# A two-layer encoder on one core: sums of the down projection moved from POOL to VectorE and to an accumulating DMA, residual added at the PSUM read, matmuls ordered bank by bank

## The chip, the cores and the metric

One core of a Trainium2 chip runs the whole program in one launch. The metric is the device time of the program in microseconds (us). The kernel before was timed in three runs: 2201.31, 2204.14 and 2206.15 us, median 2204.14 us.

## The reference, cut to what matters

Two encoder layers (a windowed attention in the first, a neighbourhood attention in the second, with memory heads beside them), each followed by a dense SwiGLU channel mixer. Everything is float32, with 1024 tokens, 1024 model columns and 2816 hidden columns. The change lies in the last product of the mixer:

```python
x = x + jnp.concatenate([y_tok, y_mem], axis=-1) @ w_out[i]
h = rmsnorm(x, norm_ffn[i])
gu = h @ w_gate_up[i]
x = x + (jax.nn.silu(gu[..., :D_FF]) * gu[..., D_FF:]) @ w_down[i]   # the down projection
```

After the second layer a final RMSNorm gives the output.

## The kernel before, in words

**Precision.** Each float32 operand is split into two reduced-precision parts: `hi` (a cast on ScalarE, ACT, L106) and `lo` (a subtraction on VectorE, DVE, L109). A product is then three matmuls: high by high, high by low, low by high (`three`).

**The down projection by seven products.** The product of a 1024x2816 weight and 2816x1024 activations is cut into halves in each direction and computed by a Strassen-like scheme of seven products instead of eight. Product `i` (0 to 6) takes a sum or difference of weight halves on the left (`left_side`) and a sum or difference of activation halves on the right. The right sides were already combined after the gate and up product, by `hand_over`, and stored to DRAM as `b_d[layer][i]` by `keep` (L963, L964). `right_side` (L1065) loads them again into `b_raw` and splits them into `hB`.

**Loops.** Each product runs over 11 row tiles `p` of the hidden dimension, taken in six groups `g` of two tiles (the last has one), and over four PSUM banks `m`. A tile and bank cost three matmuls of 128x128 by 512 columns, so a full group is 24 matmuls, one product is 132, and one layer's down projection is 924. The inner order is tile outside, bank inside, except in the last two groups, which go bank by bank (L1176 to L1187). The operands of a group are asked for two groups ahead (`dorder[at_ + 2]`).

**Weights.** `keep_rows` loads the first half-rows of the weight, both column halves, into six `wd_kept` tiles, 1 MB each (`a` and `b` are its two column halves). Product 1 needs `b` plus the second half-rows; these are loaded into a `wd_raw` tile and added on GpSimd (POOL, L1039), then DVE forms `a = b - a` (L1040). Product 3 loads two more halves and POOL subtracts them (L1061); product 5 loads one and POOL subtracts (L1050). The `wd_raw` and `xr` tiles share five slots; the split weights `wd` have three.

**Reading the banks.** At the end of products 0, 2, 3 and 4, `read` (L1094) copies each of the four banks to SBUF on ACT, loads the residual (`residual`, L1077, from `xr_d`), and adds it on POOL (L1096). In product 4 DVE also adds the copied bank to `x`. Products 1, 5 and 6 add straight from the bank on DVE. `done` squares finished tiles on ACT and sums the squares on DVE (L202) for the next RMSNorm; `scale` closes the sum with small matmuls (`st` L211, `bc` L226). In product 6 the norm of the first token half starts after group 0.

**Order.** The code is written in program order, and a scheduler lays out each engine's own instruction list from it ahead of the run: an instruction can stand earlier than its place in the text if its engine was thought to be free. On the chip each list runs strictly in order, and a list whose next instruction waits for data waits as a whole. SP issues nearly all the DMAs; ACT issues a few stores; POOL issues none.

Of the kernel before, what the change touches and what calls it, by code (L numbers as in the profile page):

```python
# [12 lines left out]
ALU = mybir.AluOpType  # L13
# [28 lines left out]
def trunk_kernel(ctx: ExitStack, tc: tile.TileContext, a: dict, out: bass.AP):  # L42
# [288 lines left out]
    for layer in range(2):  # L331
# [427 lines left out]
        with tc.tile_pool(name=f"fp{layer}", bufs=1, reuse_waits="tile") as fp:  # L759
# [203 lines left out]
            def keep(i, p, t):  # L963
                nc.sync.dma_start(b_d[layer][i][:, p * HS : (p + 1) * HS], t)  # L964
# [57 lines left out]
            def left_side(i, g):  # L1022
# [12 lines left out]
                elif i == 1:  # L1035
                    src, o = raw(), raw()
                    rows(src, g, 1, first_cols)
                    rows(o, g, 1, second_cols)
                    nc.gpsimd.tensor_tensor(b, b, o, op=ALU.add)  # L1039
# [7 lines left out]
                elif i == 5:  # L1047
                    src = raw()
                    rows(src, g, 1, first_cols)
                    nc.gpsimd.tensor_tensor(src, src, a, op=ALU.subtract)  # L1050
# [6 lines left out]
                if i == 3:  # L1057
                    r = raw()
                    rows(r, g, 0, first_cols)
                    rows(b, g, 0, second_cols)  # L1060
                    nc.gpsimd.tensor_tensor(b, r, b, op=ALU.subtract)  # L1061
# [15 lines left out]
            def residual(m, f):  # L1077
                t = raw_tile("xr")[:, :HS]
                nc.sync.dma_start(t, xr_d[layer][m][:, f * HS : (f + 1) * HS])
                return t  # L1080
# [13 lines left out]
            def read(i, m, bank):  # L1094

                add = lambda o, p_, q_, op=ALU.add, e=nc.vector: e.tensor_tensor(o, p_, q_, op=op)  # L1096
                if i == 0:
                    t = x_tile(m, 1)
                    nc.scalar.copy(t, bank)
                    add(t, t, residual(m, 1), e=nc.gpsimd)  # L1100
# [3 lines left out]
                elif i == 2:  # L1104
                    t = x_tile(m, 0)
                    nc.scalar.copy(t, bank)
                    add(t, t, residual(m, 0), e=nc.gpsimd)
                elif i == 3:
                    t = x_tile(m + 4, 0)
                    nc.scalar.copy(t, bank)  # L1110
                    add(t, t, residual(m + 4, 0), e=nc.gpsimd)
                elif i == 4:
                    t = x_tile(m + 4, 1)
                    nc.scalar.copy(t, bank)
                    add(x[m + 4][0], x[m + 4][0], t)
                    done(m + 4, 0)
                    add(t, t, residual(m + 4, 1), e=nc.gpsimd)
# [36 lines left out]
            for u, n in gate_up():  # L1154
                if u.j == NF - 1 and n in (2, 3, 4):
                    for g in (2 * n - 4, 2 * n - 3):
                        keep_rows(g)
                    if n > 2:
                        left_side(0, n - 3)
                        right_side(0, n - 3)  # L1160
# [4 lines left out]
            for at_, (i, g) in enumerate(dorder):  # L1165
                if at_ + 2 < len(dorder):
                    left_side(*dorder[at_ + 2])
                    right_side(*dorder[at_ + 2])
# [7 lines left out]
                if g == len(groups) - 1:  # L1176
                    for m in range(4):
                        product(i, m, p, bank[m])
                        read(i, m, bank[m])
                elif g == len(groups) - 2:  # L1180
                    for m in range(4):
# [105 lines left out]
```

## Time and profile before

| | us |
|---|---|
| median of three runs | 2204.14 |
| the profiled execution, its own time | 2205.49 |
| its span in the trace | 2202.5 |
| PE (TensorE matmuls) busy | 2129.8 (97%) |
| DVE busy | 1440.2 (65%) |
| ACT busy | 1056.5 (48%) |
| POOL busy | 673.9 (31%) |

The span is some 3 us less than the execution's own time. Line numbers (L1136) are those of the kernel before; a line can be a helper's. In a timeline row, "x39" means 39 merged instructions of one kind, and the bracket gives the engine's idle time ahead of them and what ended it. The down projection of the first layer runs from 850 to 1079 us of the span, that of the second from 1954 to 2181 us.

### The profile page before, as it was taken

The page shows a single profiled execution, that of the slowest core. Times are in us where ns is not written, and L with a number is a line of the kernel's source. Part 1 is how long each engine was busy: PE and PEld are TensorE (multiplying, and loading weights), DVE is VectorE, ACT ScalarE, POOL GpSimd, SP SyncE. Part 2 cuts the span into 40 slices and gives each one's busy share as a digit, 9 for nine tenths or more (in the row PEclk, how much of TensorE's full clock was granted, in tenths as well). Part 3 has the DMA queues.
Part 4 walks back from the last instruction along what each step waited for, and adds up shares of the span by engine and source line. Part 5 has one row for each costly group of instructions (what it writes and reads, how often), then busy time and mean ns, then how long its engine had stood idle before and what let it go on. Part 6 is the DMA issues. An engine that isn't in the chain of part 4 may idle for free.

```text
span 2202.5 us, 28160 instructions
## 1 busy us (share of the span) xinstructions
PE 2129.8 (97%) x9930; PEld 1749.9 (79%) x9930; DVE 1440.2 (65%) x2241; ACT 1056.5 (48%) x2016; POOL 673.9 (31%) x647
## 2 busy tenths in 40 slices
PE   6899999999999999999999999999999999999996
PEld 6688888788888887787788888887888888877875
DVE  5677787776555456767866666667865555567575
ACT  5477785443333333445466566653433333334442
POOL 4334330323332321363233233202233233213540
PEclk8999999999999999999999999999999999999998
DMA  6312117423223236766332222274232232366562
GB/s 221 119 39 82 49 58 268 133 82 122 97 93 110 100 115 225 248 208 215 111 91 72 76 65 86 64 263 139 82 101 110 96 115 96 120 225 229 178 234 81
DMA packets 117020, 287.21 MB, mean 130 GB/s; under 512 B 12304, under 2 KB 18704, under 8 KB 116880
## 3 DMA queue, kind: packets, MB, share of 16 engines
q1 hardware_dynamic: 110544, 273.89, 36.9%
q10 hardware_dynamic: 6336, 11.54, 1.4%
q8 instruction: 78, 1.28, 0.2%
q14 instruction: 62, 0.51, 0.1%
HBM read 210.40 MB, written 68.94 MB: 127 GB/s over the span
## 4 chain that ended last, share of the span: by engine, by line
PE 73%; issue 10%; DVE 6%; ACT 4%; DMA 4%; POOL 3%; SPq 0%; POOLq 0%; DVEq 0%; ACTq 0%
PE X L844 21%; PE Y L844 16%; PE mm L139 13%; PE X L1136 6%; PE po L139 4%; PE S L524 3%; PE Y L1136 3%; PE O L587 3%; PE pT L567 2%; DMA b_raw<-b_d 1%; DVE hB L109 1%; ACT p L539 1%; POOL x L1096 1%; DVE wd L109 1%; DMA wd_kept<-in_w_dn 1%
## 5 line engine op out<-in xcount | busy, mean ns | idle before, releaser
L844 PE MATMUL X<-hT,wgu 128*128 128x512 f32 x1056 | 259.0, 395 | 0.0
L844 PE MATMUL Y<-hB,wgu 128*128 128x512 f32 x1056 | 256.3, 392 | 0.0
L1136 PE MATMUL X<-hB,wd 128*128 128x512 f32 x1056 | 248.3, 395 | 7.0 <-DVE c L852 3.4
L844 PE MATMUL X<-hB,wgu 128*128 128x512 f32 x1056 | 247.8, 390 | 0.0
L1136 PEld LDWEIGHTS X<-hB,wd 128*128 128x128 f32 x1056 | 200.2, 190 | 52.9 <-DVE c L852 4.3
L844 PEld LDWEIGHTS X<-hT,wgu 128*128 128x128 f32 x1056 | 198.2, 188 | 47.2
L552 POOL TENSOR_SCALAR p<-p,stat 128x384 f32<-128x384 f32 (+1 forms) x256 | 140.9, 570 | 309.8 <-DVE stat L549 206.6
L844 PEld LDWEIGHTS Y<-hB,wgu 128*128 128x128 f32 x1056 | 198.5, 188 | 43.9 <-issue 1.5
L844 PEld LDWEIGHTS X<-hB,wgu 128*128 128x128 f32 x1056 | 198.3, 188 | 41.8
L106 ACT CAST wgu<-wS 128x1024 fp32r<-128x1024 f32 x88 | 92.5, 1051 | 259.7 <-POOL wS L803 157.1
L109 DVE TENSOR_TENSOR wgu<-wgu_raw,wgu 128x1024 fp32r<-128x1024 f32 (+1 forms) x88 | 85.7, 974 | 190.3 <-ACT wgu L106 190.3
L139 PE MATMUL mm<-hT,wqk 128*128 128x512 f32 x672 | 199.8, 405 | 0.1
L1136 PE MATMUL Y<-hB,wd 128*128 128x512 f32 x792 | 185.2, 395 | 8.9 <-DVE hB L109 4.5
L803 POOL TENSOR_TENSOR wS<-wgu_raw 128x512 f32<-128x512 f32 x44 | 73.6, 1672 | 379.0 <-DVE wgu L109 379.0
L139 PE MATMUL po<-yT,wo 128*128 128x512 f32 x768 | 184.7, 394 | 0.0
L1136 PEld LDWEIGHTS Y<-hB,wd 128*128 128x128 f32 x792 | 150.6, 191 | 42.6 <-DVE hB L109 5.3
L109 DVE TENSOR_TENSOR hB<-b_raw,hB 128x512 fp32r<-128x512 f32 x154 | 131.9, 892 | 53.1 <-ACT hB L106 52.9
L139 PEld LDWEIGHTS po<-yT,wo 128*128 128x128 f32 x768 | 142.4, 188 | 29.5 <-issue 1.0
L109 DVE TENSOR_TENSOR wgu<-wS,wgu 128x1024 fp32r<-128x1024 f32 x88 | 109.7, 1247 | 62.6 <-ACT wgu L106 62.6
L539 ACT ACTIVATE p<-p,stat 128x256 f32<-128x256 f32 (+1 forms) x192 | 112.4, 586 | 51.1 <-DVE stat L535 48.5
L810 POOL TENSOR_TENSOR wS<-wgu_raw 128x512 f32<-128x512 f32 x44 | 58.3, 1326 | 251.2 <-DMA wgu_raw<-in_w_gu 197.5
L106 ACT CAST hB<-b_raw 128x512 fp32r<-128x512 f32 x154 | 88.8, 619 | 95.4 <-DMA b_raw<-b_d 95.3
(158 smaller groups left out, 4026.8 us busy)
## 6 DMA issues: line engine op xcount, KB each, us to landing
wgu_raw<-in_w_gu SPq DMA_DIRECT2D x92, 512.0 KB
b_raw<-b_d SPq DMA_DIRECT2D x70, 512.0 KB
wd_raw<-in_w_dn SPq DMA_DIRECT2D x50, 512.0 KB
b_d<-c SPq DMA_DIRECT2D x88, 256.0 KB
b_d<-t SPq DMA_DIRECT2D x66, 256.0 KB
wo_raw<-in_w_out SPq DMA_DIRECT2D x32, 512.0 KB
wd_kept<-in_w_dn SPq DMA_DIRECT2D x10, 1024.0 KB
x<-in_x SPq DMA_DIRECT2D x32, 256.0 KB
```

Of the source, the lines that this page charges most:

```text
L106: nc.scalar.copy(dst, src)
L109: (eng or nc.vector).tensor_tensor(dst, src, h.bitcast(F32), op=ALU.subtract)
L139: nc.tensor.matmul(ps[:, :n], l, r, start=start and i == 0 and j == 0, stop=stop and i == len(order) - 1 and j == 2,)
L524: nc.tensor.matmul(s_[:, :n], Q[self.h][:, qb * P : (qb + 1) * P], k, start=j == 0, stop=j == 1)
L539: nc.scalar.activation(p[:, :n], p[:, :n], AF.Exp, bias=m1, scale=-1.0, accum_out=s1)
L552: nc.gpsimd.tensor_scalar(p[:, :n], p[:, :n], ri[:, i : i + 1], 1.0, op0=ALU.mult, op1=ALU.mult)
L567: nc.tensor.transpose(tr[:, j * P : (j + 1) * P], p[:, j * P : (j + 1) * P], ident)
L587: nc.tensor.matmul(o[:, c0 : c0 + w * P], self.value(j), t[:, s0 : s0 + w].rearrange("p j q -> p (j q)"), start=j == js[0] and t is self.p ...
L803: sub = lambda o, p_, q_: nc.gpsimd.tensor_tensor(o, p_, q_, op=ALU.subtract)
L810: nc.gpsimd.tensor_tensor(s[:, HS:], u1, u2, op=ALU.add)
L844: nc.tensor.matmul(ps, l, r, start=n in (0, 1, 3, 6) and k == 0 and i == 0, stop=k == 3 and i == 2, skip_group_check=True,)
L1136: nc.tensor.matmul(bank, l, r, start=i in (0, 1, 3, 6) and p == 0 and n == 0, stop=p == HF - 1 and n == 2, skip_group_check=True,)
```

## The change

1. `left_side`, product 1: the second half-rows are no longer loaded into a tile and added on POOL. A DMA issued from POOL's queue adds them into `b` while it writes (`accum_op=ALU.add`).
2. `left_side`, products 5 and 3: the two subtractions move from POOL to DVE.
3. `residual`: the residual tiles of four banks are loaded ahead, at group 3 of products 0, 2, 3 and 4, by two DMAs of two tiles each; the sixteen loads per layer become eight.
4. `read`: no copy on ACT and no addition on POOL. DVE adds bank and residual in one instruction. In product 4 DVE reads each bank twice.
5. `keep`: the seven stores of the last row tile (`p == HF - 1`) are issued from POOL's queue, not SP's.
6. The right side of product 0, group 2, is asked for inside the gate and up loop, with groups 0 and 1, and no longer after it.
7. Every group runs bank by bank (bank outside, tile inside).
8. In product 6 the norm of the first half starts after group 1, not 0, and the squares of the other half are added one group later.

```diff
             def keep(i, p, t):
-                nc.sync.dma_start(b_d[layer][i][:, p * HS : (p + 1) * HS], t)
+                queue = nc.gpsimd if p == HF - 1 else nc.sync
+                queue.dma_start(b_d[layer][i][:, p * HS : (p + 1) * HS], t)
...
                 elif i == 1:
-                    src, o = raw(), raw()
+                    src = raw()
                     rows(src, g, 1, first_cols)
-                    rows(o, g, 1, second_cols)
-                    nc.gpsimd.tensor_tensor(b, b, o, op=ALU.add)
+                    nc.gpsimd.dma_start(
+                        b, wd[p : p + n, 1].rearrange("n r c -> r n c")[:, :, second_cols], accum_op=ALU.add
+                    )
                     nc.vector.tensor_tensor(a, b, a, op=ALU.subtract)
...
                 elif i == 5:
                     src = raw()
                     rows(src, g, 1, first_cols)
-                    nc.gpsimd.tensor_tensor(src, src, a, op=ALU.subtract)
+                    nc.vector.tensor_tensor(src, src, a, op=ALU.subtract)
...
-                    nc.gpsimd.tensor_tensor(b, r, b, op=ALU.subtract)
+                    nc.vector.tensor_tensor(b, r, b, op=ALU.subtract)
...
-            def residual(m, f):
-                t = raw_tile("xr")[:, :HS]
-                nc.sync.dma_start(t, xr_d[layer][m][:, f * HS : (f + 1) * HS])
-                return t
+            residuals = {}
+
+            def residual(i):
+
+                if i in (0, 2, 3, 4):
+                    m0, f = {0: (0, 1), 2: (0, 0), 3: (4, 0), 4: (4, 1)}[i]
+                    for m in range(m0, m0 + 4, 2):
+                        t = raw_tile("xr").rearrange("p (n c) -> p n c", c=HS)
+                        nc.sync.dma_start(
+                            t, xr_d[layer][m : m + 2].rearrange("m p t -> p m t")[:, :, f * HS : (f + 1) * HS]
+                        )
+                        residuals[m, f], residuals[m + 1, f] = t[:, 0], t[:, 1]
...
                 if i == 0:
-                    t = x_tile(m, 1)
-                    nc.scalar.copy(t, bank)
-                    add(t, t, residual(m, 1), e=nc.gpsimd)
+                    add(x_tile(m, 1), bank, residuals.pop((m, 1)))
...
                 elif i == 4:
-                    t = x_tile(m + 4, 1)
-                    nc.scalar.copy(t, bank)
-                    add(x[m + 4][0], x[m + 4][0], t)
+                    add(x[m + 4][0], bank, x[m + 4][0])
+                    add(x_tile(m + 4, 1), bank, residuals.pop((m + 4, 1)))
                     done(m + 4, 0)
-                    add(t, t, residual(m + 4, 1), e=nc.gpsimd)
...
+                if u.j == NF - 1 and n in (3, 4, 5):
+                    right_side(0, n - 3)
...
-                    right_side(*dorder[at_ + 2])
+                    if at_ > 0:
+                        right_side(*dorder[at_ + 2])
...
-                if g == len(groups) - 1:
-                    for m in range(4):
-                        product(i, m, p, bank[m])
+                if g == 3:
+                    residual(i)
+                for m in range(4):
+                    for q in range(n):
+                        product(i, m, p + q, bank[m])
+                    if g == len(groups) - 1:
                         read(i, m, bank[m])
-                elif g == len(groups) - 2:
-                    for m in range(4):
-                        for q in range(n):
-                            product(i, m, p + q, bank[m])
-                else:
-                    for q in range(n):
-                        for m in range(4):
-                            product(i, m, p + q, bank[m])
-                if i == 6:
-                    if g == 0:
+                if i == 6 and g > 0:
+                    if g == 1:
                         parts = norms[0].split(1, hT[0]) if is_a else finish(norms[0], 0)
                     run_some(parts, 2)
-                    if g < 4:
-                        norms[1].add(x[g][1], g)
+                    if g < 5:
+                        norms[1].add(x[g - 1][1], g - 1)
```

Products 2 and 3 are read in the same new way as product 0.

## Rows read from the trace of the kernel before

**Rows 1.** Stretch of the first layer, L1136 alone: length, PE, PEld busy (count), clock, DMA.

```profile
850.00:1079.00 229.00, 215.93 (x924) 175.65 (x924) 0.98 0.60 208
```

**Rows 2.** Stretches, all engines: PE, PEld, DVE, ACT, POOL busy, clock, DMA share, GB/s.

```profile
850.00:870.00 20.00, 16.42 (x63) 12.43 (x62) 13.83 (x17) 5.85 (x8) 0.25 (x1) 0.91 0.91 331
1050.00:1070.00 20.00, 20.00 (x77) 15.85 (x77) 14.46 (x23) 8.51 (x15) 1.94 (x1) 0.83 0.31 113
850.00:1079.00 229.00, 218.57 (x938) 177.90 (x937) 164.99 (x170) 100.60 (x155) 79.36 (x41) 0.98 0.60 208
```

**Rows 3.** PE's timeline, first layer: start, length, what [idle before, releaser].

```profile
850.34 2.20 PE L1136 MATMUL X<-hB,wd 128*128 128x512 f32 x9
854.32 10.74 PE L1136 MATMUL X<-hB,wd 128*128 128x512 f32 x39 [1.78 <-DVE c L852]
866.72 19.77 PE L1136 MATMUL X<-hB,wd 128*128 128x512 f32 x84 [1.66 <-ACT hB L106]
...
904.71 13.67 PE L1136 MATMUL Y<-hB,wd 128*128 128x512 f32 x59 [1.68 <-DVE hB L109]
918.22 30.08 PE L1136 MATMUL X<-hB,wd 128*128 128x512 f32 x132
948.14 30.08 PE L1136 MATMUL Y<-hB,wd 128*128 128x512 f32 x132
...
1026.56 13.44 PE L1136 MATMUL Y<-hB,wd 128*128 128x512 f32 x58 [1.65 <-DVE wd L109]
...
1049.77 1.45 PE L211 MATMUL st<-inv_d,sq 128*128 128x1 f32 x8 [3.43 <-DVE sq L202]
...
1056.41 22.22 PE L1136 MATMUL X<-hB,wd 128*128 128x512 f32 x94
```

**Rows 4.** PE's timeline, second layer.

```profile
1954.13 2.20 PE L1136 MATMUL X<-hB,wd 128*128 128x512 f32 x9
1957.97 9.18 PE L1136 MATMUL X<-hB,wd 128*128 128x512 f32 x39 [1.63 <-DVE c L852]
1968.80 19.77 PE L1136 MATMUL X<-hB,wd 128*128 128x512 f32 x84 [1.65 <-ACT hB L106]
...
2007.91 15.31 PE L1136 MATMUL Y<-hB,wd 128*128 128x512 f32 x59 [2.79 <-DVE hB L109]
...
2127.53 20.51 PE L1136 MATMUL Y<-hB,wd 128*128 128x512 f32 x82 [2.65 <-DVE wd L109]
...
2159.45 21.44 PE L1136 MATMUL X<-hB,wd 128*128 128x512 f32 x92
```

**Rows 5.** DVE's timeline around the start of the first down projection.

```profile
847.89 3.44 DVE L1040 TENSOR_TENSOR wd_kept<-wd_kept 128x1024 f32<-128x1024 f32 x1
...
854.19 1.21 DVE L1040 TENSOR_TENSOR wd_kept<-wd_kept 128x1024 f32<-128x1024 f32 x1
```

**Rows 6.** SP's queue, the same stretch: issues only.

```profile
838.08 7.34 SPq L1020 DMA_DIRECT2D wd_kept<-in_w_dn  x6
...
853.70 2.66 SPq L964 DMA_DIRECT2D b_d<-c  x2
...
859.35 0.44 SPq L1068 DMA_DIRECT2D b_raw<-b_d  x1
```

**Rows 7.** Chain of waits, 834 to 870 us: start, length, what.

```profile
838.08 5.04 DMA wd_kept<-in_w_dn
```

**Rows 8.** Groups by line and form, 845 to 1080 us: count | busy, mean ns | idle before.

```profile
L109 DVE TENSOR_TENSOR hB<-b_raw,hB 128x512 fp32r<-128x512 f32 x73 | 65.7, 938 | 23.2 <-ACT hB L106 23.2
L109 DVE TENSOR_TENSOR wd<-wd_kept,wd 128x1024 fp32r<-128x1024 f32 x20 | 31.9, 1593 | 20.6 <-ACT wd L106 20.6
...
L1096 DVE TENSOR_TENSOR x<-Y,x 128x512 f32<-128x512 f32 x8 | 5.1, 683 | 0.0
...
L1096 POOL TENSOR_TENSOR x<-x,xr 128x512 f32<-128x512 f32 x16 | 29.1, 1842 | 54.6 <-ACT x L1099 35.2 <-DVE x L1096 19.5
...
L1061 POOL TENSOR_TENSOR wd_kept<-wd_raw,wd_kept 128x1024 f32<-128x1024 f32 x5 | 13.0, 2609 | 44.7 <-DMA wd_kept<-in_w_dn 44.7
```

More of the change, by code (lines that the diff above doesn't have):

```diff
@@ L1094, in read @@
             def read(i, m, bank):
-                add = lambda o, p_, q_, op=ALU.add, e=nc.vector: e.tensor_tensor(o, p_, q_, op=op)
+                add = lambda o, p_, q_, op=ALU.add: nc.vector.tensor_tensor(o, p_, q_, op=op)
                 if i == 0:
-                    t = x_tile(m, 1)
-                    nc.scalar.copy(t, bank)
-                    add(t, t, residual(m, 1), e=nc.gpsimd)
+                    add(x_tile(m, 1), bank, residuals.pop((m, 1)))
                 elif i == 1:
@@ L1104, in read @@
                 elif i == 2:
-                    t = x_tile(m, 0)
-                    nc.scalar.copy(t, bank)
-                    add(t, t, residual(m, 0), e=nc.gpsimd)
+                    add(x_tile(m, 0), bank, residuals.pop((m, 0)))
                 elif i == 3:
-                    t = x_tile(m + 4, 0)
-                    nc.scalar.copy(t, bank)
-                    add(t, t, residual(m + 4, 0), e=nc.gpsimd)
+                    add(x_tile(m + 4, 0), bank, residuals.pop((m + 4, 0)))
                 elif i == 4:
-                    t = x_tile(m + 4, 1)
-                    nc.scalar.copy(t, bank)
-                    add(x[m + 4][0], x[m + 4][0], t)
+                    add(x[m + 4][0], bank, x[m + 4][0])
+                    add(x_tile(m + 4, 1), bank, residuals.pop((m + 4, 1)))
                     done(m + 4, 0)
-                    add(t, t, residual(m + 4, 1), e=nc.gpsimd)
                 elif i == 5:
@@ L1159, in trunk_kernel @@
                         left_side(0, n - 3)
-                        right_side(0, n - 3)
+                if u.j == NF - 1 and n in (3, 4, 5):
+                    right_side(0, n - 3)
             norms = [Norm(), Norm()]
```

## The prediction

> **What bounds the kernel now.** I read the shares of the page first: PE is busy for 97% of the span, so only a stretch where PE stands still or runs at its lower clock can be shortened. Then the stretch of L1136 in the first layer, which holds 924 matmuls in 229 us [rows 1]; the second layer has as many. The timeline of PE gives the price of one matmul when nothing disturbs: product 2 starts at 918.22 and product 3 at 948.14 us, so 132 matmuls take 29.92 us, 0.2267 us each [rows 3]. 924 of them need 209.4 us. From 850.34 to the end of the last piece at 1056.41 + 22.22 = 1078.6 us are 228.3 us in the first layer [rows 3], and from 1954.13 to 2180.9 us 226.8 us in the second [rows 4]. I leave 1.5 us per layer for the norm's own small matmuls (eight of them are the 1.45 us piece at 1049.77 us). The excess is 17.4 + 15.9 = 33.3 us. That is all PE can get back in this phase.
>
> The same rows say where it lies, as start-to-start time less 0.2267 us per matmul between:
>
> - Start (first 48 matmuls): 850.34 to 866.72 us, 16.4 for 10.9, 5.5 lost; second layer 3.8. The idle parts are 1.78 us for DVE's `c` (the fourth bank is not yet read) and 1.66 us for `hB` of group 2; the second layer repeats both with 1.63 and 1.65. The rest is clock: 0.91 granted in 850 to 870 us [rows 2], that is some matmuls at 1.2 instead of 2.4 GHz after the idle time.
> - Product 1, group 3, `hB` late: to 904.71 us, 157 matmuls, 2.4 lost; second layer 3.5 [rows 3, 4].
> - Product 5, DVE's `wd` late: up to 1026.56 us 1.8 lost; second layer, from 2007.91 to 2127.53 us, 505 matmuls in 119.6 us, 5.1 lost, part of it slow clock behind the 2.79 us idle ahead.
> - The norm inside product 6: 3.43 us idle for the sum of squares, then a clock of 0.83 in 1050 to 1070 us [rows 2]. From 1026.56 to 1056.41 us are 96 matmuls, 29.9 us for 21.8 and the norm's 1.5, so 6.6 lost, and 0.9 in the last piece; second layer 2.8 and 0.6, mostly the clock after its 2.65 us idle.
>
> **Why DVE is late.** The same subtraction L1040 takes 3.44 us at 847.89 and 1.21 us at 854.19 us [rows 5]; in the first case POOL was adding L1039 beside it. So over the stage: `hB` has a mean of 938 ns where a 512-column addition from PSUM has 683 [rows 8]. POOL is busy for 79 us of the 229 [rows 2]. A POOL sum thus costs its own time and slows DVE two- to threefold while it lasts.
>
> **Part by part, one layer.**
>
> POOL's 18 weight sums and 16 residual sums go. What DVE no longer pays is at least 73 x (0.938 - 0.683) = 18.6 us on `hB` and 20 x (1.593 - 1.21) = 7.7 us on the kept weights, 26 us [rows 5, 8]. What DVE takes over: 12 subtractions (10 x 1.21 + 2 x 0.68 = 13.5 us) and 16 additions from PSUM (10.9 us by the 683 ns row), 24.4 us. DVE stays near 163 of the 229 us, but without the threefold stretches. Product 5 is the tightest: twelve 1024-column operations less the half-size ones (12.5), eleven `hB` (7.5 at 683 ns), and up to twelve 512-column reads and square sums (8.2) make 28 us in a product of 29.9. So DVE just keeps up there, and a short wait in product 5 may stay.
>
> ACT's 16 copies go; ACT is busy for 101 of 229 us and no stall above ends on it alone, so I cost this at nothing.
>
> The start. With bank outside, the fourth bank is wanted after 18 matmuls instead of 9, 2.0 us later, more than the 1.78 us idle; and without POOL's sum DVE's L1040 gives 2.2 us back ahead of `c`. This stall goes. `hB` of group 2 is late because SP stood in order behind the seven stores of the last tile: it could issue the first of these only at 853.70 us, when DVE had made its data, and so `b_raw` at 859.35 us [rows 6]. After the change the stores wait on POOL's queue, where nothing on PE's path but the accumulating DMAs can stand behind them, and `b_raw` is asked for right behind the kept weights, whose six issues end at 845.4 us [rows 6]. It lands behind 5.8 MB of these at 331 GB/s [rows 2], about 857 us by estimate, and is split by 860, before PE wants it at 861. I take 8 of the 9.3 us of both layers.
>
> The accumulating DMA. No DMA of the kernel before comes from POOL's queue or adds, so its price isn't in the trace. From below: nothing, or the wait of POOL's sum saved, if it lands as soon as a plain load would: 1 MB landed in 5.04 us [rows 7], and POOL's sum could begin no sooner than its load was in. From above: L1040 stands in DVE's list in front of the work that frees the fourth bank. If it waits for the DMA, DVE waits as a whole, `g` and `c` with it; each us past about 849.5 us is one us of PE. I take a landing some 6 us after issue, near the 5.04 row, and 1 us of PE per layer, since the scheduler may place L1040 later now; the upper ends are the first and the fourth rival.
>
> Product 1 and its neighbours: `hB` and `wd` no longer wait for threefold operations, and SP no longer waits for POOL to free `wd_raw` and `xr` slots. I take 5.5 of 5.9 us. Against it, bank outside wants the second tile of a group after 3 matmuls instead of 12, 2.0 us earlier; where DVE is ahead by a group this costs nothing. Product 5: 5 of 6.9 us. The subtraction of product 3 on DVE waits for a DMA that POOL waited for with 44.7 us of idle time [rows 8]; if DVE's list has it too early, it costs up to the 5 us of a load once or twice, covered by the two groups (10.9 us) that are asked for ahead.
>
> The norm of product 6: started 24 matmuls later, 5.4 us, more than the 3.43 us idle. 8 of 10.9 us; the tail of product 6 still has to end before its next user, and the last norm behind the final matmul is not touched.
>
> The residual loads are the same bytes in half the issues, ahead of need: nothing.
>
> Sum: 8 + 5.5 + 5 + 8 = 26.5 us back, 2 us lost to the new DMA, -24.5 us. 2205.5 - 24.5 = 2181.0 us on the profiled execution's own time, which is 1.35 us above the median, so **2180 us** in the median.
>
> **The Trainium skill against it.** SP's `b_raw` was issued only at 859.35 us although the DMA engines ran at 0.91 of their time [rows 2, 6]. "DMA: Bandwidth & Descriptors", section "Issuing engines are not separate DMA queues", says that transfers started by any engine share the same 16 DMA engines, so that another queue saves issue time alone; and "Collectives: The Full Stack", section "The bandwidth ceiling: the fold count and why AG ≠ RS ≠ AR", that an adding transfer reads two sources and so moves at half the rate. No row shows an adding transfer. By both, the sums come in the one stretch where the engines are full, which is the first rival.
>
> **Rivals.**
>
> 1. *The sums collide with the start.* Each kept tile lands from 843 us on, and its sum can start at once. If a 0.5 MB sum takes as long as the plain 1 MB load, 5 us, and shares with kept weights and `b_raw`, the group 2 wait stays and L1040 is some 3 to 4 us late. The start then gives nothing back (8 us less) and costs about 2 us a layer more: 2180 + 12 = 2192 us. For it: 0.91 of DMA time. Against: kept loads are issued first.
> 2. *The stalls only move.* DVE at 28 of 29.9 us in product 5, DMA waits in its list, and the earlier need of the second tile make new stalls of 2 to 3 us with the slow clock behind them, in two or three places a layer: some 20 us of the 26.5 are given back, 2200 to 2204 us, no change. Against: POOL is gone from 79 us.
> 3. *All of it comes back*: PE runs dry nowhere, 2205.5 - 33.3, about 2171 us.
> 4. *Slower: DVE stands behind a slow sum.* If the first sum lands at 873 us, 30 us after its issue, PE waits some 23 us and 2 us of slow clock in each layer, 50 us, less the 21 us of the other parts: 2235 us. It decides from a landing about 860 us, where 2 x 10.5 us equal those 21; that is 17 us after issue, more than three times the 5.04 us of a load twice the size. For it: nothing of the kind was ever run here, and each of six sums gates a subtraction.
>
> "The change doesn't do what it says" would be that L1040 of later groups sits in DVE's list where the sums of the POOL list stand behind the seven stores (about 859 us): these stores' data then gate the sums, which is a form of the fourth.
>
> **Numbers.** Forecast 2180 us, its own range 2172 to 2190: 0.58. First rival 0.15, second 0.09, third 0.05, fourth 0.13. About 0.2% (4.4 us) is what a measurement can tell from no change. Faster: 0.58 + 0.15 + 0.05 less a little for the first's upper end, 0.77; same: 0.10, the second; slower: 0.13, the fourth. The range goes from the third rival's side, 2169, to the lower end of the second, 2203 us; what lies beyond is mainly the fourth.
>
> **What would show it.** POOL with next to no busy time between 850 and 1079 us; every `hB` split near 0.68 us and every L1040 near 1.21; no ACT copies. PE's first piece runs to 18 matmuls and more without a wait for `c`; `b_raw` of group 2 issued about 845 us; the `st` piece with no idle ahead. Each down projection some 214 to 217 us long, the rest of the program as before. It is wrong if DVE idles for an accumulating DMA near 848 us, if PE's waits in product 5 are still over 2 us, or if the two stretches are not shorter by 20 us together.

## The result, and the profile after

The changed kernel takes 2213.49 us in the median of 6 runs (2210.28 to 2216.98), the kernel before 2203.42 us (2201.31 to 2206.15): a ratio of 1.0045 [1.0032, 1.0058]. It is slower by 10 us, where 24 us less were forecast. Its profiled execution took 2211.3 us, with a span of 2209.5 us. All times below are medians of undisturbed executions: one of the four of plain_load_stores_on_sp took 2627.02 us at a granted clock of 0.75 and is left out.

The timeline of PE in both down projections (the matmuls of L1136 have become L1138) answers to [rows 3, 4]; columns are start, length, what, idle before and its releaser:

```profile
847.64 4.24 PE L1138 MATMUL X<-hB,wd 128*128 128x512 f32 x18
855.87 2.93 PE L1138 MATMUL X<-hB,wd 128*128 128x512 f32 x6 [4.00 <-DVE c L852]
862.48 0.80 PE L1138 MATMUL X<-hB,wd 128*128 128x512 f32 x1 [3.68 <-ACT hB L106]
870.82 26.31 PE L1138 MATMUL X<-hB,wd 128*128 128x512 f32 x107 [7.54 <-DVE hB L109]
896.96 30.08 PE L1138 MATMUL Y<-hB,wd 128*128 128x512 f32 x132
...
1046.56 11.05 PE L1138 MATMUL X<-hB,wd 128*128 128x512 f32 x48
1057.45 0.95 PE L211 MATMUL st<-inv_d,sq 128*128 128x1 f32 x8
...
1061.07 18.29 PE L1138 MATMUL X<-hB,wd 128*128 128x512 f32 x78
...
1954.52 4.24 PE L1138 MATMUL X<-hB,wd 128*128 128x512 f32 x18
1963.61 2.93 PE L1138 MATMUL X<-hB,wd 128*128 128x512 f32 x6 [4.85 <-DVE c L852]
1969.15 0.49 PE L1138 MATMUL X<-hB,wd 128*128 128x512 f32 x1 [2.61 <-ACT hB L106]
1978.26 27.25 PE L1138 MATMUL X<-hB,wd 128*128 128x512 f32 x107 [8.62 <-DVE hB L109]
2005.34 30.08 PE L1138 MATMUL Y<-hB,wd 128*128 128x512 f32 x132
...
2169.44 18.29 PE L1138 MATMUL X<-hB,wd 128*128 128x512 f32 x78
```

Two things are to be seen. From product 1 on, no piece has an idle time any more: products 1 to 5 take 1046.56 - 896.96 = 149.60 us, which is 660 matmuls at 0.2267 us, and the norm's `st` piece begins without a wait. And the whole loss now lies in product 0: from 847.64 to 896.96 us are 49.3 us for work of 29.9, 19.4 lost, and from 1954.52 to 2005.34 us 50.8 us, 20.9 lost. Before, the start lost 5.5 and 3.8 us. So the account is 13.9 + 17.1 = 31.0 us more at the start. Behind it, the first projection (231.7 us, less 209.4 and 1.5 for the norm) loses 1.4 us where it lost 11.9, the second 1.4 where it lost 12.1: 21.2 us came back. The net is +9.8 us, close to the 10 us between the medians. The two traces by themselves differ by 7.0 us only (2209.5 against 2202.5): the first down projection begins 2.7 us earlier here, and this lead is there within the first 200 us of the program, which the change does not touch (a granted clock of 0.96 against 0.93 there). Each kernel was profiled once.

DVE's timeline in that stretch says why. L1042 is the subtraction that was L1040 in [rows 5]:

```profile
851.66 1.23 DVE L1042 TENSOR_TENSOR wd_kept<-wd_kept 128x1024 f32<-128x1024 f32 x1 [8.00 <-DMA wd_kept<-in_w_dn]
...
855.14 0.68 DVE L852 TENSOR_TENSOR c<-c,X 128x512 f32<-128x512 f32 x1
858.09 1.23 DVE L1042 TENSOR_TENSOR wd_kept<-wd_kept 128x1024 f32<-128x1024 f32 x1 [2.27 <-DMA wd_kept<-in_w_dn]
...
868.94 1.23 DVE L1042 TENSOR_TENSOR wd_kept<-wd_kept 128x1024 f32<-128x1024 f32 x1 [3.75 <-DMA wd_kept<-in_w_dn]
870.08 3.69 DVE L109 TENSOR_TENSOR hB<-b_raw,hB 128x512 fp32r<-128x512 f32 x6
```

The subtraction itself takes 1.23 us each time, as forecast, but DVE stands in front of it for 8.00, 2.27 and 3.75 us, each time until an accumulating DMA has landed. Everything behind it waits along: `c`, which frees the fourth bank, comes at 855.14 us, and DVE's part of six `hB` only at 870.08. ACT had cast the first two of these, group 1, at 861.81 us, and those of group 2 at 868.37:

```profile
861.81 1.14 ACT L106 CAST hB<-b_raw 128x512 fp32r<-128x512 f32 x2 [1.88 <-DMA b_raw<-b_d]
868.37 1.14 ACT L106 CAST hB<-b_raw 128x512 fp32r<-128x512 f32 x2 [5.42 <-DMA b_raw<-b_d]
```

POOL's queue and SP's (SPq, issues only):

```profile
840.41 1.25 POOL L1039 DMA_DIRECT2D wd_kept<-in_w_dn x1 [8.67 <-DMA wd_kept<-in_w_dn]
...
846.59 1.20 POOL L1039 DMA_DIRECT2D wd_kept<-in_w_dn x1 [1.64 <-DMA wd_kept<-in_w_dn]
855.53 0.59 POOL L965 DMA_DIRECT2D b_d<-c x1 [7.74 <-DVE c L852]
856.10 1.21 POOL L1039 DMA_DIRECT2D wd_kept<-in_w_dn x1
860.22 0.62 POOL L965 DMA_DIRECT2D b_d<-c x1 [2.90 <-DVE c L852]
...
863.71 2.18 POOL L1039 DMA_DIRECT2D wd_kept<-in_w_dn x2
```

```profile
831.50 0.42 SPq L1070 DMA_DIRECT2D b_raw<-b_d  x1
834.73 7.95 SPq L1021 DMA_DIRECT2D wd_kept<-in_w_dn  x6
842.73 0.43 SPq L1070 DMA_DIRECT2D b_raw<-b_d  x1
...
843.71 29.20 SPq L1070 DMA_DIRECT2D b_raw<-b_d  x6
```

The kernel before, SP's issue of the right side of group 1 and ACT's casts of group 2:

```profile
834.85 0.42 SPq L1068 DMA_DIRECT2D b_raw<-b_d  x1
```

```profile
866.05 1.14 ACT L106 CAST hB<-b_raw 128x512 fp32r<-128x512 f32 x2
```

The first sum was issued at 840.41 and landed for DVE at 851.66 us, 11.2 us. The fourth stands in POOL's list behind a store that waits for `c` (7.74 us), `c` waits for DVE, and DVE waits for the first sum: a chain through three queues, so the fourth is issued only at 856.10 and the last two at 863.71 us. On SP, the right side of group 1 is asked for at 842.73, behind the six kept weights; before it went out at 834.85 us, ahead of them. ACT waited 1.88 us for it; that is the 3.68 us idle of PE at 862.48. The right side of group 2 was asked for at 843.71 us, 16 us sooner than before [rows 6], and yet reached ACT at 868.37, where before it was there by 866.05.

The DMA engines in the same stretch (DMA view, 836 to 900 us: queue, packets, MB, share of 16 engines' time; then one issue group with its median time to landing), and PE, PEld, DVE, ACT, POOL, clock, DMA share and GB/s in two slices of 5 us, to set beside [rows 2]:

```profile
q1 hardware_dynamic: 3618, 11.86, 50.2%
q0 software_dynamic: 1984, 4.46, 30.5%
...
wd_kept<-in_w_dn POOLq DMA_DIRECT2D x5, 512.0 KB, 14.2
```

```profile
855.00:860.00 5.00, 2.93 (x6) 1.82 (x6) 2.73 (x5) 1.13 (x2) 1.79 (x2) 0.50 1.08 293
...
865.00:870.00 5.00, 0.00 (x0) 0.00 (x0) 1.25 (x2) 1.14 (x2) 0.90 (x1) 0.50 1.05 351
```

The engines are full (1.02 to 1.08 in every slice from 835 to 875 us), POOL's queue q0 takes 30.5% of their time for 4.46 MB, and the matmuls behind PE's first wait run at a granted clock of 0.50, the lower level of 1.2 GHz.

Away from the start the forecast signs are there. The groups of DVE from 845 to 1060 us, against [rows 8]:

```profile
L109 DVE TENSOR_TENSOR hB<-b_raw,hB 128x512 fp32r<-128x512 f32 x72 | 46.2, 686 | 12.9 <-ACT hB L106 12.7
...
L1042 DVE TENSOR_TENSOR wd_kept<-wd_kept 128x1024 f32<-128x1024 f32 x5 | 6.1, 1226 | 14.1 <-DMA wd_kept<-in_w_dn 14.0
```

`hB` takes 686 ns in the mean where it took 938. The 14.0 us idle ahead of L1042 are the sum of the three waits above.

### The profile page after: what moved, and what is told of

It is laid out like the page before. It is cut to its first block, busy times and chain, and to the rows that moved or that the text cites. A ratio compares the mean times of both kernels' runs of the same rounds, so it can differ in the third digit from the quotient of the medians.

```text
span 2209.5 us, 28042 instructions
## 1 busy us (share of the span) xinstructions
PE 2124.1 (96%) x9930; PEld 1746.7 (79%) x9930; DVE 1406.0 (64%) x2297; ACT 1042.0 (47%) x1984; POOL 546.4 (25%) x605
## 4 chain that ended last, share of the span: by engine, by line
PE 73%; issue 16%; DVE 3%; ACT 3%; DMA 3%; POOL 2%; POOLq 0%; SPq 0%; DVEq 0%; ACTq 0%
PE X L844 21%; PE Y L844 16%; PE mm L139 14%; PE X L1138 5%; PE Y L1138 4%; PE po L139 4%; PE S L524 3%; PE O L587 3%; PE pT L567 3%; DMA b_raw<-b_d 1%; ACT p L539 1%; DMA wd_kept<-in_w_dn 1%; PE bc L226 1%; DVE pl L109 1%; DVE sq L202 0%
## 5 line engine op out<-in xcount | busy, mean ns | idle before, releaser
L1138 PE MATMUL X<-hB,wd 128*128 128x512 f32 x1056 | 251.5, 399 | 31.3 <-DVE hB L109 16.2
L1138 PEld LDWEIGHTS X<-hB,wd 128*128 128x128 f32 x1056 | 202.7, 193 | 77.6 <-DVE hB L109 17.0
L1138 PE MATMUL Y<-hB,wd 128*128 128x512 f32 x792 | 180.5, 389 | 0.0
L1138 PEld LDWEIGHTS Y<-hB,wd 128*128 128x128 f32 x792 | 148.7, 188 | 30.9
L803 POOL TENSOR_TENSOR wS<-wgu_raw 128x512 f32<-128x512 f32 x44 | 73.6, 1672 | 377.5 <-DVE wgu L109 377.5
L139 PEld LDWEIGHTS po<-yT,wo 128*128 128x128 f32 x768 | 142.4, 188 | 29.6 <-issue 1.0
L217 POOL TENSOR_TENSOR nr<-nv,neg_half 128x4 f32<-128x4 f32 (+1 forms) x11 | 10.9, 989 | 523.7 <-DVE nv L216 517.8
L109 DVE TENSOR_TENSOR pl<-pT,ph 128x384 fp32r<-128x384 f32 (+1 forms) x256 | 119.0, 494 | 23.5 <-ACT ph L106 20.2
```

The costliest lines, as they stand in the source:

```text
L109: (eng or nc.vector).tensor_tensor(dst, src, h.bitcast(F32), op=ALU.subtract)
L139: nc.tensor.matmul(ps[:, :n], l, r, start=start and i == 0 and j == 0, stop=stop and i == len(order) - 1 and j == 2,)
L803: sub = lambda o, p_, q_: nc.gpsimd.tensor_tensor(o, p_, q_, op=ALU.subtract)
L1138: nc.tensor.matmul(bank, l, r, start=i in (0, 1, 3, 6) and p == 0 and n == 0, stop=p == HF - 1 and n == 2, skip_group_check=True,)
```

## The experiments

The theory after the result: the accumulating DMAs do it, by DVE standing in order behind them and by their share of full DMA engines, made worse by the stores on POOL's queue. The main rival: the residual additions at the PSUM read, the bank order or the many operations on DVE cost the time. Edits are to the changed kernel unless said otherwise; each ratio is to the kernel before on the same chip. The runs were made on several chips; the kernel before has medians of 2203.4 to 2204.5 us there, so differences between runs hold to a microsecond or two.

### The accumulating DMA alone: accumulate_alone

The kernel before, with nothing but L1039 replaced:

```diff
-                    src, o = raw(), raw()
+                    src = raw()
                     rows(src, g, 1, first_cols)
-                    rows(o, g, 1, second_cols)
-                    nc.gpsimd.tensor_tensor(b, b, o, op=ALU.add)
+                    nc.gpsimd.dma_start(b, wd[...][:, :, second_cols], accum_op=ALU.add)
```

> The kernel before with one part of the change alone: the first sum by the accumulating DMA from POOL's queue; POOL keeps its other sums, stores and order as before. Theory A (the DMA lands some 11 us after its issue among the kept weights, and DVE stands behind it in order): the wait for c at the start grows from 1.8 to 6 us or more in each layer, and slow clock behind it; part of the waits in product 1 goes with POOL's sums. 2208 to 2222 us, slower than before. Rival: the harm needs the other parts (seven stores on POOL's queue between the sums, right side of group 1 behind the kept weights), then this part alone is within 4 us of before.

Measured: 2220.27 us, 1.0072 [1.0056, 1.0087]. This part alone makes the kernel slower, by more than the whole change does, although POOL's sums for product 1 are gone. DVE waits for the first sum, PE for `c` and then for `hB`:

```profile
854.43 1.23 DVE L1041 TENSOR_TENSOR wd_kept<-wd_kept 128x1024 f32<-128x1024 f32 x1 [7.90 <-DMA wd_kept<-in_w_dn]
858.65 11.68 PE L1137 MATMUL X<-hB,wd 128*128 128x512 f32 x39 [6.34 <-DVE c L852]
875.94 21.77 PE L1137 MATMUL X<-hB,wd 128*128 128x512 f32 x84 [5.62 <-ACT hB L106]
```

The stores are still on SP here, so neither they nor the residual part is needed for the loss.

### A plain load and an addition on DVE in its place: plain_load_dve_add

```diff
-                    nc.gpsimd.dma_start(b, wd[...][:, :, second_cols], accum_op=ALU.add)
+                    o = raw()
+                    rows(o, g, 1, second_cols)
+                    nc.vector.tensor_tensor(b, b, o, op=ALU.add)
```

> The kernel after with the first sum by a plain load on SP into a wd_raw tile, as before, and the addition on DVE. DVE has six more additions per layer (6.7 us by 1.21 us each). Theory A: no accumulating DMA, no wait of DVE in front of c except for a load that was asked for ahead of the kept weights; the c wait goes: 2180 to 2192 us. Theory B: b_raw of group 1 still stands behind the kept weights: 2192 to 2200 us. If the sum's place in time makes no difference at all: 2210 us or more.

Measured: 2185.30 us, 0.9912 [0.9897, 0.9927]. All other parts of the change stay, and the 28 us between this and the changed kernel go with the accumulating DMA. What is left in product 0 is a wait of 2.42 us for a right side.

### The sums held back until the rush is over: held_sums

A one-element operation on DVE that reads a later right side (`held`, times 0, added to `b`) must be done before the sum may start, and the subtraction moves to the preparation of product 2:

```diff
+                    held = right[0, 8][:, 1, 0:1].bitcast(F32)
+                    nc.vector.scalar_tensor_tensor(b[:, 0, 0:1], held, 0.0, b[:, 0, 0:1], op0=ALU.mult, op1=ALU.add)
                     nc.gpsimd.dma_start(b, ..., accum_op=ALU.add)
-                    nc.vector.tensor_tensor(a, b, a, op=ALU.subtract)
                 elif i == 2:
+                    held = right[1, 2 * min(g + 3, 5)][:, 1, 0:1].bitcast(F32)
+                    one = sp.tile([P, 1], F32, tag="one", name="one", bufs=2)
+                    nc.vector.tensor_scalar(one, held, 0.0, 1.0, op0=ALU.mult, op1=ALU.add)
+                    nc.vector.scalar_tensor_tensor(a, b, one, a, op0=ALU.mult, op1=ALU.subtract)
```

> The kernel after, but the six accumulating DMAs may start only when hB of group 4 of product 0 is split (a one-element DVE operation on b carries the dependence), and DVE's subtraction a = b - a stands in product 2, behind hB of product 1. Same bytes, same queue, later. Theory A (DVE stands in its own order behind an accumulating DMA issued into full DMA engines): the 8 us wait of DVE goes, the wait for c goes, most of the 19 to 21 us lost in product 0 of each layer comes back, 2176 to 2186 us. Theory B (the right side of group 1 is late because its load stands behind 5.8 MB of kept weights): only the c wait goes, b_raw of group 1 is still late, some 10 us per layer stay, about 2193 to 2200 us.

Measured: 2183.87 us, 0.9905 [0.9890, 0.9920]. With the six sums and the subtraction behind them later, the time is that of the plain load (2185.3): it was their place that cost the time. The sums are not free even there: with the stores on SP in both, the kernel with held sums takes 4 us more than the one with plain loads (2179.68 against 2175.56, below). Product 0 still takes 35.1 us, with one wait of 3.20 us for the right side of group 1.

### Sums early, subtraction late: early_sums_late_subtraction

The second half of the edit above without the first: the sums run in the rush, but DVE does not stand behind them.

> The kernel after with its accumulating DMAs issued as early as there; only DVE's subtraction a = b - a is held back into product 2, so that nothing in DVE's list waits for a sum near the start. If DVE standing in order is the larger cause: no wait for c, and hB of group 1 late only by its load, 2188 to 2196 us. If the sums' share of the full DMA engines is the larger cause: b_raw of group 1 lands at the same late time as after (14 us behind the start of product 0) and PE waits as long for it, 2202 to 2212 us.

Measured: 2197.25 us, 0.9964 [0.9953, 0.9976], between the two expectations: no wait for `c` is left, as the first said, and the right side of group 1 is as late as in the changed kernel, as the second said. Of the 2213.5 - 2183.9 = 29.6 us, 16 go when DVE no longer stands behind the sums, 13 only when the sums leave the rush. PE's timeline shows the second part by itself:

```profile
847.92 5.60 PE L1141 MATMUL X<-hB,wd 128*128 128x512 f32 x24
862.06 27.63 PE L1141 MATMUL X<-hB,wd 128*128 128x512 f32 x108 [8.54 <-ACT hB L106]
889.53 15.80 PE L1141 MATMUL Y<-hB,wd 128*128 128x512 f32 x69
```

PE waits 8.54 us for the right side of group 1. ACT gets it at 861.39 us, where it got it at 861.81 in the changed kernel; both have it behind the kept weights in SP's list, among the sums. Product 0 takes 41.6 us: 7.7 less than in the changed kernel, 6.5 more than with the sums held.

### The addition left out: no_adding

```diff
-                        b, wd[...][:, :, second_cols], accum_op=ALU.add
+                        b, wd[...][:, :, second_cols]
```

> The kernel after with the same DMA from POOL's queue at the same place, but a plain copy into b: the addition of the two weight halves is left out. If adding is what makes the DMA slow, the landing of a 512 KB transfer falls from 14 us to 5 or 6 and DVE's first wait from 8 us to about 2: 2190 to 2198 us. If the full DMA engines make it slow (theory A as told, whatever the DMA does), the landing stays at 9 us or more and the time at 2203 to 2213 us.

Measured: 2197.87 us, 0.9964 [0.9952, 0.9976], 16 us below the changed kernel. A copy of the same bytes from the same queue lands in 8.9 us instead of 14.2, later than the 5 or 6 us expected (DMA view, 834 to 905 us):

```profile
wd_kept<-in_w_dn POOLq DMA_DIRECT2D x5, 512.0 KB, 8.9
```

So about half of the loss hangs on the adding itself, the other half on a transfer in that place that DVE waits for: DVE still waits 4.80 us, PE 5.42 and 2.43 us for `hB`.

### The stores back on SP: stores_on_sp

```diff
-                queue = nc.gpsimd if p == HF - 1 else nc.sync
+                queue = nc.sync
```

> The kernel after with the seven stores of the last row tile back on SP's queue; b_raw of group 1 then stands ahead of the kept weights in SP's list again, and the six accumulating DMAs follow each other on POOL's queue with no store between them. Theory A: DVE's first wait for the sum stays at 6 to 9 us, PE's wait for c stays near 4 us, so at most some 10 us of 2213 go: 2200 to 2212 us. Theory B: the waits for hB of group 1 (11 us in each layer) go, 2188 to 2196 us.

Measured: 2200.59 us, 0.9984 [0.9974, 0.9993]. 13 us come back: PE no longer waits for the right side of group 1, and DVE's second and third waits fall to 1.07 and 1.90 us, with no store between the sums in POOL's list. DVE's first wait stays at 8.20 us and PE's for `c` at 4.65, so the chain through POOL's queue is not what makes the first sum late. Here q0 carries nothing but the sums, which gives their price (same view and stretch):

```profile
q1 hardware_dynamic: 5725, 15.93, 62.6%
q0 software_dynamic: 1504, 2.88, 22.0%
...
wd_kept<-in_w_dn POOLq DMA_DIRECT2D x5, 512.0 KB, 13.0
```

0.220 x 71 us / 2.88 MB = 5.4 us of all 16 engines for 1 MB of sums, 0.626 x 71 / 15.93 = 2.8 us for 1 MB of plain transfers: 1.94 times as much.

### Right sides of groups 0 and 1 ahead of the kept weights: right_first_only

```diff
             for u, n in gate_up():
+                if u.j == NF - 1 and n == 2:
+                    right_side(0, 0)
+                    right_side(0, 1)
...
-                if u.j == NF - 1 and n in (3, 4, 5):
+                if u.j == NF - 1 and n == 5:
                     right_side(0, n - 3)
```

> The kernel after, where the right sides of groups 0 and 1 are asked for ahead of the kept rows; sums and subtractions as after. If DVE standing in order is the larger cause: the wait for c stays at 4 us or grows and a late split of weights or right sides behind it stays, 2203 to 2211 us. If the late load of group 1 is the larger one: 2188 to 2198 us.

Measured: 2206.45 us, 1.0009 [0.9998, 1.0020]: 7 us back, and the waits behind DVE stay, as the timeline of PE shows:

```profile
849.76 4.24 PE L1138 MATMUL X<-hB,wd 128*128 128x512 f32 x18
857.92 10.47 PE L1138 MATMUL X<-hB,wd 128*128 128x512 f32 x34 [3.91 <-DVE c L852]
873.74 6.49 PE L1138 MATMUL X<-hB,wd 128*128 128x512 f32 x21 [5.35 <-DVE hB L109]
```

The wait for group 1 is gone; those for `c` and for `hB` of a later group are there.

### The residual part alone: residual_at_psum_only

The kernel before, with the residual loaded in pairs and added at the PSUM read, and no ACT copies; weight sums and stores as before:

```diff
-                    t = x_tile(m, 1)
-                    nc.scalar.copy(t, bank)
-                    add(t, t, residual(m, 1), e=nc.gpsimd)
+                    add(x_tile(m, 1), bank, residuals.pop((m, 1)))
```

> The kernel before with the residual part alone: loads ahead, DVE adds bank and residual, no copy on ACT, no residual sum on POOL; weight sums stay on POOL. If POOL's residual sums (16 a layer, slots of wd_raw held until they are done) are what made the waits in products 1 and 5 and at the norm: 10 to 18 us less, 2186 to 2194 us. If POOL's weight sums made them: within 4 us of before.

Measured: 2184.83 us, 0.9912 [0.9888, 0.9935]: this part alone gives 20 us. That is more than the 10 to 18 us expected. POOL is busy for 44.8 of the 212 us from 850 to 1062 us (before 73.3), and the mean of `hB` falls from 955 ns in this stretch to 767. ACT's copies and the late loads go in the same run, so it does not show that POOL's sums alone made the difference.

### The weight sums alone, all on DVE: weight_sums_on_dve_only

The kernel before, with `nc.vector` for `nc.gpsimd` in L1039, L1050 and L1061; loads, residual and stores as before:

```diff
-                    nc.gpsimd.tensor_tensor(b, b, o, op=ALU.add)
+                    nc.vector.tensor_tensor(b, b, o, op=ALU.add)
```

> The kernel before with all three weight sums on DVE (plain loads, no accumulating DMA); residual sums stay on POOL, order as before. If POOL's weight sums made the waits in products 1 and 5: 8 to 16 us less, 2188 to 2196 us. If the residual sums made them, DVE has 18 more operations per layer and still stands beside POOL: 2200 to 2208 us.

Measured: 2184.12 us, 0.9907 [0.9883, 0.9932]: 20 us again, more than the 8 to 16 expected. POOL keeps 16 residual sums (29.5 us), and `hB` has a mean of 822 ns, yet PE has no idle time in products 1 to 5. Either half of the relief by itself takes away most of DVE's lateness, so the two gains don't add up: the best run of all has 28 us.

### Two of the three weight sums back on POOL: held_pool_subtractions

held_sums, with the subtractions for products 3 and 5 on `nc.gpsimd` again.

> held_sums with the subtractions of products 3 and 5 back on POOL (12 per layer, some 2.4 us each when undisturbed). If a POOL sum slows DVE two- to threefold while it runs and that made the waits in product 5 of the kernel before, DVE's operations in products 3 and 5 show 1.7 to 3.4 us again and PE waits 1.5 to 3 us in product 5: 2186 to 2192 us. If the residual sums on POOL were what hurt, or DVE has room enough now, the time stays at 2182 to 2186 us.

Measured: 2186.33 us, 0.9923 [0.9906, 0.9940], against 2183.87 for held_sums: too close to tell apart. The waits expected in product 5 did not come; product 4 has one of 0.54 us. DVE is slowed all the same, as expected. The splits of the kept weights, 850 to 1062 us, in held_sums and then in this run:

```profile
L109 DVE TENSOR_TENSOR wd<-wd_kept,wd 128x1024 fp32r<-128x1024 f32 x18 | 21.9, 1219 | 10.8 <-ACT wd L106 10.8
L109 DVE TENSOR_TENSOR wd<-wd_kept,wd 128x1024 fp32r<-128x1024 f32 x18 | 29.0, 1613 | 9.9 <-ACT wd L106 9.9
```

Only POOL's subtractions differ between the two, so this is the cleanest sign that a POOL sum slows DVE. With the residual off POOL, DVE has room enough for it.

### The old inner order, and the old start of the norm: held_tile_outside, held_norm_at_group_0

Both are made from held_and_stores_on_sp (below). The first puts the tile loop outside the bank loop again, the second starts the norm at group 0 of product 6 (`if i == 6:` with `g == 0` and `x[g]`, for `if i == 6 and g > 0:`).

> held_and_stores_on_sp with the inner order of the kernel before (tile outside, bank outside only in the last two groups). The prediction held that bank outside buys 2.0 us at the start, when the fourth bank is wanted. If so, PE waits for c again after 9 matmuls, by 1 to 2 us, in each layer: 2182 to 2187 us. If DVE, free of POOL, has c ready in time anyway, the order is worth nothing: 2178 to 2181 us.

> held_and_stores_on_sp with the norm inside product 6 started after group 0 as in the kernel before. If its later start was needed, PE waits again for the sum of squares, 1 to 3.5 us in one or both layers and slow clock after it: 2182 to 2190 us. If DVE, free of POOL, has the sum ready by then, the start is worth nothing: 2178 to 2181 us.

Measured: 2180.03 us, 0.9894 [0.9878, 0.9911], and 2179.44 us, 0.9889 [0.9874, 0.9903], where the kernel they come from has 2179.68. With a DVE that keeps up, neither the bank order nor the norm's later start is worth anything that can be measured: PE does not wait for `c` in either order, and the `st` piece has no idle time at either place. What they would be worth with a late DVE was not run.

### Mending the rest of the start: held_and_stores_on_sp, held_and_right_first, spread_sums

held_sums with the stores on SP; held_sums with the right sides ahead; and the first of these with the sums released one by one through product 1:

```diff
-                    held = right[0, 8][:, 1, 0:1].bitcast(F32)
+                    held = (right[1, 2 * g - 2] if g else right[0, 10])[:, 1, 0:1].bitcast(F32)
```

> held_sums with the stores of the last row tile on SP, by which b_raw of group 1 stands ahead of the kept weights in SP's list. Theory A with the list order as second cause: the 3.2 us idle for hB of group 1 that held_sums had left goes, with the slow clock behind it: 4 to 6 us per layer less, 2172 to 2178 us. If the stores on SP hold back the next right sides (as in the kernel before), a wait of 1.5 to 3 us for hB of group 2 or 3 takes its place: 2180 to 2186 us.

> held_sums with the stores on POOL's queue, and the right sides of groups 0 and 1 asked for before the kept rows in the program, by which b_raw of group 1 is issued behind the first kept tile only. Expected: PE runs through product 0 with no wait over 1 us; 5 us per layer less than held_sums, 2171 to 2177 us. If the late b_raw is not the cause of the 3.2 us, the time stays at 2184 us.

> held_and_stores_on_sp, but the six accumulating DMAs are let go one after the other through product 1 (each behind the split of a later hB) instead of all six at once in product 0's end. If the 1.5 to 2.5 us idle for hB of group 1 of product 1 comes from six accumulating DMAs filling the engines at once, it goes: 2 to 5 us per layer less, 2171 to 2177 us, and the median landing falls from 9 us or more to 5 or 6. If each lands as late as before, DVE stands in product 1 or 2 for it: 2180 us or more.

Measured: 2179.68 us, 0.9889 [0.9874, 0.9904]; 2183.21 us, 0.9904 [0.9885, 0.9923]; 2180.48 us, 0.9891 [0.9874, 0.9908]. Product 0 runs in its 29.9 us in all three. All three miss the lower times expected: a wait for a later right side, loaded while the sums run, has come instead. In held_and_right_first the wait of 3.20 us in product 0 goes, as was hoped, and the time stays at that of held_sums. That the sums hold up these right sides is the likely reason; plain_load_stores_on_sp (below), without sums, has no such wait. PE's timeline of held_and_stores_on_sp in product 1:

```profile
878.87 5.60 PE L1143 MATMUL Y<-hB,wd 128*128 128x512 f32 x24
885.97 0.50 PE L1143 MATMUL Y<-hB,wd 128*128 128x512 f32 x1 [1.50 <-ACT hB L106]
```

held_and_right_first has 2.34 us in that place, and spread_sums 0.99 us later in product 1 and 1.84 us at the start of product 2, for its own gate.

### No DMA from POOL's queue at all: plain_load_stores_on_sp

plain_load_dve_add with the stores on SP as well.

> plain_load_dve_add with the stores of the last row tile on SP: no DMA at all from POOL's queue. b_raw of group 1 stands ahead of the kept weights, no accumulating DMA is left, POOL and the port are free. If the order of the loads was what was left of plain_load_dve_add (2.3 us idle per layer plus slow clock), 2174 to 2181 us, as good as the held accumulating DMA; if six more DVE additions or SP standing for the stores cost, 2182 to 2188 us.

Measured: 2175.56 us, 0.9866 [0.9850, 0.9882], the best of all, ahead of the kernel before by 28 us and of the changed one by 38. PE's timeline of the first down projection:

```profile
850.39 30.08 PE L1138 MATMUL X<-hB,wd 128*128 128x512 f32 x132
...
1044.39 18.25 PE L1138 MATMUL X<-hB,wd 128*128 128x512 f32 x78
```

850.39 to 1062.64 us are 212.3 us for 209.4 us of matmuls and the norm: all but 1.4 us of the excess is gone. Against plain_load_dve_add (2185.30), the stores on SP are worth some 10 us even with no sum in flight: the right side of group 1 goes out at 834.90 us again, ahead of the kept weights at 838.13.

## Why the prediction was wrong

**The step that failed is the price of the accumulating DMA** ("I take a landing some 6 us after issue, near the 5.04 row, and 1 us of PE per layer"). The sum has it at 2 us for both layers. By itself on the kernel before it costs 17 us (accumulate_alone), and in the changed kernel 28 us against a plain load. In the sum's own terms the start was to be 8 - 2 = 6 us shorter and is 31.0 us longer; that turns -24.5 into +9.8. The first sum took 11.2 us, and the median of the five of 512 KB is 14.2. The forecast took its price from a plain load of 1 MB that led the queue. In the rush, a plain copy of half the bytes takes 8.9 us (no_adding), and adding takes the engines 1.94 times the time. The Trainium skill, in "Collectives: The Full Stack", section "The bandwidth ceiling: the fold count and why AG ≠ RS ≠ AR", says of a collective's adding step that it reads two sources and so runs at half the rate of a copy. The 1.94 measured here agrees; the prediction cited this and left it to its first rival.

**The hope that "the scheduler may place L1040 later" failed too.** L1042 stayed ahead of `g` and `c` in DVE's list. early_sums_late_subtraction prices this: with the subtraction out of DVE's way, 16 us come back.

**The first rival was the right place and too small; the fourth was the right mechanism with a wrong turning point.** The first gave up the start's 8 us and took 2 us a layer. The fourth let DVE stand behind the first sum only, so that it decided from a landing 17 us after issue. (Its "21 us of the other parts" are 5.5 + 5 + 8 = 18.5 by the prediction's own terms, which makes it some 16 us.) In fact 11 us were enough, since DVE stood three times (8.00, 2.27, 3.75 us) and the right sides were late besides. The form that the prediction named last, sums of later groups behind the stores in POOL's list, happened also: the fourth sum waits behind a store for 7.74 us.

**The start** ("8 of the 9.3 us of both layers"). That "`b_raw` is asked for right behind the kept weights" came true: group 2's went out at 843.71 us, with 845 forecast. But it reached ACT at 868.37 us, where the estimate had it landed at 857. And with the stores gone from SP, the list put group 1's behind the weights too, which the prediction did not see. The sentence that nothing on PE's path but the sums can stand behind the stores overlooked that the sums are enough. right_first_only gives 7 us of it back, stores_on_sp 13. The section "Issuing engines are not separate DMA queues" of the Trainium skill's "DMA: Bandwidth & Descriptors" says that starting DMAs from another engine saves issue time only, since all share the same 16 DMA engines. The trace fits: the share is 1.02 or more in every slice from 835 to 875 us, and in the changed kernel, with the sums among them, the right sides of groups 1 and 2 came no sooner.

**Behind the start it was right, for more than it needed.** Product 1, product 5 and the norm were to give 5.5 + 5 + 8 = 18.5 us and gave 21.2; every `hB` is near 0.69 us. The reason given, POOL's sums slowing DVE, is borne out: by weight_sums_on_dve_only and residual_at_psum_only, each worth 20 us (the second takes off other work too), and by the splits in held_pool_subtractions. But two more reasons that the forecast gave are worth nothing measurable once DVE keeps up: the bank order (2.0 us claimed at the start) and the norm's later start (5.4 us claimed). The DVE load that the second rival feared (28 of 29.9 us in product 5) made no wait.

**The floor held.** No run went below the third rival's 2171 us; plain_load_stores_on_sp, 4.6 us above it, shows that 28 of the 33.3 us could be had together. One small slip in the account: the loss in product 5 of the first layer is 1.9 us by its own rows, not 1.8.

Not settled: the 13 us that early sums cost without DVE's waits are measured with group 1's right side behind the kept weights. What they would cost with it ahead is open, as no run has early sums and a free DVE together with the stores on SP.

## What to carry to other kernels

Here an operation that waited for a DMA took its whole engine along: before a subtraction is made to depend on a transfer, look at what stands behind it in the engine's list, and price the transfer by what lands in that same stretch, not by one that had the engines to itself. With full DMA engines, the accumulating transfers cost more than the additions they saved: second plain loads and 1.2 us of DVE for each sum beat them by 28 us. Moving the stores to another queue also re-ordered the loads that stayed, so read both lists again.

## What the hardware showed that was not expected

- An accumulating DMA took 1.94 times the engine time per MB of plain transfers beside it (5.4 against 2.8 us of 16 engines), and landed 9.6 us (held_sums, median) to 16.4 us (early_sums_late_subtraction, median) after issue for 512 KB.
- POOL spent 1.2 us on the issue of one such sum, 0.7 us on a plain copy in its place (no_adding) and 0.6 us on a store, where SP spent 0.3 us on the same store and 0.4 us on a load of 512 KB.
- POOL's sums slow DVE (1219 to 1613 ns in the mean of the kept weights' splits), and yet matter little once DVE has some lead: with the residual off POOL, the weight sums of products 3 and 5 back on POOL left PE one wait of 0.54 us in the first layer (held_pool_subtractions).
